# Masked-score products of a state-space mixer: two heads alternating, piece by piece, in place of one head at a time

## Chip, cores and metric

The kernel runs on one core of a Trainium2 chip, in one launch. The metric is the device time of one execution in microseconds; the time of a kernel is the median of its runs.

## What is computed

A block of two layers on 512 tokens (256 of context, 256 latent) of width 1024, each layer a mixer and a convolutional feed-forward network. The first mixer is gated linear attention beside an mLSTM, the second, where the change lies, a bidirectional state-space mixer: 32 heads of 64 channels in 4 groups, whose B and C have a state of 128. Cut to what matters:

```python
def odd_mixer(hc, hl, ...):
    fc = odd_features(hc, ...)          # z, x, B, C, dt of the context
    fl = odd_features(hl, ...)          # the same of the latent tokens
    yc, yl = bidir_scan(scan_f, scan_b, ...)
    ...
# one step of a scan, in one direction:
#   y[t] = sum over s <= t of (C[t] . B[s]) exp(cum[t] - cum[s]) dt[s] x[s]
#        + exp(cum[t]) C[t] . state
```

The kernel takes the 256 latent tokens as one piece in each direction. For a head, the masked scores times the decays form a matrix of keys by queries, and the values `dt[s] x[s]` (64 channels) are multiplied with it. This product is what the change reorders.

## The kernel before

The weights come as blocks of 128 x 128 in transfers of 1 MB on SyncE's queue. Each half of a transfer is split into a high part (ScalarE, L168) and a low part (VectorE or GpSimd, L169), and each block gives three products on TensorE (`mm3`, L180 to L182). The order of the work on each engine is the order in which a scheduler puts the program's instructions, from code written in stages.

`odd_mixer` (L921) works through the 32 heads in 16 chunks of two heads. Five stages run with lags, so that each step of the loop at L1134 holds parts of three chunks:

- `start` (step's own chunk) calls `project`: x through a convolution (ScalarE L949 and L952, VectorE L336, L337 and L953) and z through a gate (L1046, L1047); 16 blocks of weights, 48 products.
- `tokens` (the chunk before): x token-major (transposing products, L1057), weighted for the end state of the context (`xw`, L1062) and by dt (`xd`, L1063), the product for the end state (L1066) and its copy `S` (ScalarE, L1068).
- `outputs` (two chunks before): the products of masked scores with values (L1114), then VectorE adds the part from the end states and multiplies with the gate (L1116, L1117), and ScalarE squares (L1120) for the norm. The squares of a group of four chunks are summed by GpSimd (L1122); after the fourth they go through `colsum` (L127), Newton steps on VectorE and `spread` (L135).
- `decays` (the chunk before): the decays between tokens, `G`, on ScalarE (L1084, L1087) and VectorE (L1086, L1088), from rows that a transfer spreads over all partitions (L1077).
- `inter` (the chunk before): the products with the end states (L1100), then VectorE (L1101) and GpSimd (L1102, L1103).

`PARTS` (L25) lists the pieces of the causal matrices: a direction, the tile of 128 keys, and the queries from and to. Of the four pieces two have 256 queries and two have 128. In `outputs` each head has these four products; they add up in one region of PSUM, partitions 0 to 63 for the chunk's first head and 64 to 127 for its second, in a bank (`vps`) of which there is one only, and which `inter` uses too. The products of L1114 are of 128 keys by 64 channels, in plain float32.

Two other places matter below. `mod_part` (L243) computes shift and scale of a norm: eight products (L249), each with 32 output rows, and product k adds into the quarter k % 4 of the partitions. After the chunks come the high and low parts of y (L1143 on ScalarE, L1144 on VectorE) and the out-projection; where there is room the scheduler puts pieces of both beside the last chunks.

Of the kernel before, what the change touches and what calls it, by code (L numbers as in the profile page):

```python
# [16 lines left out]
P = 128  # L17
D = 1024
KD = 8
TL = 256  # L20
T = 512
SEGS = ((0, 0, 256), (1, 256, 512))
EPS = 1e-6
# causal pieces of a 256-token segment, keys in tile t: (direction, t, queries from, to, mask column, offset)
# [27 lines left out]
def block_kernel(ctx: ExitStack, tc: tile.TileContext, A: dict, out: bass.AP):  # L52
    nc = tc.nc
    PSUM = bass.MemoryType.PSUM
# [53 lines left out]
    def rsqrt(ss, scale, eps):  # L108
        """(ss * scale + eps) ** -0.5 of a few columns, by Newton steps from the exponent's halving"""
        n = ss.shape[-1]  # L110
        m, y, w = (np_.tile([P, 16], F32, tag=t, name=nm(t), bufs=2)[:, :n] for t in ("rm", "ry", "rw"))
        v.tensor_scalar(out=m, in0=ss, scalar1=scale, scalar2=eps, op0=ALU.mult, op1=ALU.add)
        v.tensor_scalar(out=w.bitcast(I32), in0=m.bitcast(I32), scalar1=1, scalar2=None, op0=ALU.logical_shift_right)
        v.tensor_scalar(out=y.bitcast(I32), in0=w.bitcast(I32), scalar1=-1.0, scalar2=1597463007.0, op0=ALU.mult, op1=ALU.add)
        for _ in range(3):
            v.tensor_tensor(out=w, in0=y, in1=y, op=ALU.mult)
            v.scalar_tensor_tensor(out=w, in0=w, scalar=-0.5, in1=m, op0=ALU.mult, op1=ALU.mult)
            v.scalar_tensor_tensor(out=y, in0=w, scalar=1.5, in1=y, op0=ALU.add, op1=ALU.mult)
        return y

    def colsum(sq, c=0, ps=None):
        """column sums of sq [128, n] with the columns on partitions: [128, n / 128] of a PSUM tile"""
        nt = sq.shape[-1] // P
        ps = vps() if ps is None else ps
        for t in range(nt):
            # each product overwrites all but the first column of the one before
            te.matmul(out=ps[:, c + t:c + t + P], lhsT=sq[:, t * P:(t + 1) * P], rhs=ones[:, :P], start=True, stop=True)  # L127
        return ps[:, c:c + nt]

    def spread(col, out):  # L130
        """out[:, t] = col[t % 128, t // 128] on every partition"""
        nt = col.shape[-1]
        ps = vps()[:, :nt * P]
        for t in range(nt):
            te.transpose(ps[:, t * P:(t + 1) * P], col[:, t:t + 1].to_broadcast([P, P]), ident)  # L135
        s.copy(out=out, in_=ps)

# [1 line left out]
    class Stream:  # L139
        def __init__(self, src, nblocks, fill=None, every=1, skip=0, ahead=1, pool=rawp, eng=lambda u: v):  # L140
            """fill: other work, one piece of it put ahead of every `every`-th transfer's products;
            ahead: how many splits run ahead of the products; eng: what computes the low parts"""
# [5 lines left out]
        def load(self, d):  # L148
            """transfer d to its place in SBUF"""
            if self.rawi != d:  # L150
                w = min(16, self.n - d * 16) * P
                self.raw = self.pool.tile([P, 2048], F32, tag="raw", name=nm("raw"))
                # the first transfer in halves, its second one with its split
# [30 lines left out]
    def gemm_f(st, b0, nk, acts, c0=0, c1=T, bank=gps, ks=None):  # L184
        """feature-major: [128 columns of W, tokens c0:c1]"""
# [7 lines left out]
    def gemm_k(st, b0, nk, acts, spans, pss=None, ks=None):  # L193
        """as gemm_f for a few column tiles at once (blocks [k][tile]), so that products start with the first k"""
# [12 lines left out]
    def gemm_t(st, b0, nk, acts, tiles):  # L207
        """token-major: [128 tokens, 512 columns of W] per token tile"""
# [21 lines left out]
    def mod_chunk(l, j, pool=rawp, psa=vps, tag="raw", n=2, bufs=None):  # L230
        """512 of the vectors' columns, their weights in n transfers"""
# [11 lines left out]
    def mod_part(q, pool, psa):  # L243
        """as mod_chunk, 256 columns of the first layer's mixer norm"""
# [8 lines left out]
    def mod_out(l, c, n, ps, psa):  # L253
        """add up the quadrants, with the columns on partitions: n tiles of 128 columns from tile c"""
# [10 lines left out]
        if i in (1, 4):  # L265
            # (1 + scale) * gain, in place of scale
# [4 lines left out]
    class Norm:  # L271
        """1 / rms over the features of tokens c0:c1, a feature tile at a time"""
# [17 lines left out]
        def cols(self):  # L290
            """[token % 128, token tile]"""
            return rsqrt(self.most, 1.0 / D, EPS)

        def row(self):
            """on all partitions, the tokens along the free axis"""
# [29 lines left out]
    # residual: x += gate * y  # L325
# [6 lines left out]
    def conv_side(y, ps, w0, w2):  # L332
        """the two outer taps of a width-3 convolution within each segment"""
# [12 lines left out]
    def warm(n, rhs):  # L346
        """products of ones, so that the tensor engine keeps its clock up while the first data come"""
# [3 lines left out]
    with tc.tile_pool(name="stp", bufs=6) as stp:  # L351
# [13 lines left out]
        def start(k, acts):  # L365
            # the first products run as their K tiles come, between the parts of shift and scale
# [35 lines left out]
    with ExitStack() as st:  # L402
# [6 lines left out]
        def turn(k):  # L409
            """the gain, then token-major"""  # L410
# [29 lines left out]
def even_mixer(E, st, acts, pss0, then):  # L440
# [52 lines left out]
    # log_sigmoid(x) = min(x, 0) - ln(1 + exp(-|x|)), each table loaded once  # L493
# [60 lines left out]
    # token-major columns: [t, tile, row of RQ], and the end-state weights of the context  # L554
# [30 lines left out]
    for j in range(2):  # L585
# [51 lines left out]
        # end state of the context, both directions  # L637
# [22 lines left out]
        # outputs, token-major, and their norm per head  # L660
# [28 lines left out]
    # q and k carry a factor 2 each from the tanh form of silu  # L689
# [4 lines left out]
    def head(h):  # L694
# [5 lines left out]
        # end state of the context: [k, value | norm] per direction  # L700
# [15 lines left out]
        for sg in range(2):  # L716
# [4 lines left out]
            # [s, t] weights: forward s0 -> t 0:256, s1 -> t 128:256; backward s0 -> t 0:128, s1 -> t 0:256  # L721
# [28 lines left out]
    def finish(h):  # L750
        # output gate (twice it), norm, transposed
# [53 lines left out]
def conv_ffn(E, st, l, acts, fill, then):  # L805
# [20 lines left out]
    def around(y, ps, ti):  # L826
        """the other taps"""
# [15 lines left out]
    # VectorE keeps to one operand from SBUF where GpSimd works beside it  # L843
# [3 lines left out]
    def project(j):  # L847
# [5 lines left out]
        elif not full:  # L853
            # a pair to a bank; the others hold sums of the down-projection
# [3 lines left out]
        else:  # L858
            # the down-projection takes the usual banks before the last two are through
# [9 lines left out]
    for hf in range(nh):  # L869
# [6 lines left out]
        for jj in range(per):  # L876
# [4 lines left out]
            # the down-projection's first columns, as far as their K tiles are there  # L881
# [4 lines left out]
            if jj == per - 2 and not full:  # L886
                # and a column more while the last pairs are convolved
# [25 lines left out]
        if full and last:  # L913
            # the last two a segment at a time, so that the next norm starts on the first
# [6 lines left out]
def odd_mixer(E, st, acts, then):  # L921
# [13 lines left out]
    # dt, B, C, B: the context first, C without it  # L935
# [8 lines left out]
    def conv_silu(b0, ti, out, c0):  # L944
        """out = 2 silu(conv + bias)"""
# [13 lines left out]
    def group(q):  # L959
# [5 lines left out]
        # x and B each carry a factor 2  # L965
# [6 lines left out]
        # [s, dir, 384]: forward s0 x t 0:256, s1 x t 128:256; backward s1 x t 0:256, s0 x t 0:128  # L972
# [12 lines left out]
    # softplus(x) = max(x, 0) + ln(1 + u), u = exp(-|x|), with the rounding of 1 + u put back  # L985
# [24 lines left out]
    # token-major: context w_end = exp(c_end - cum) dt [s, dir*32 + head]; latent cum and dt  # L1010
# [7 lines left out]
    tok = T_([P, 2, P], "tokc")     # [s, tile, cum (64) | dt (64)]  # L1018
# [33 lines left out]
    def tokens(i):  # L1052
        """token-major x: context weighted for the end state, latent by dt, per direction; D x"""
# [4 lines left out]
        xw = T_([P, 2, 2, 2, 64], "xw", pool=sp)    # [s, tile, dir, head, 64]  # L1058
        xd = T_([P, 2, 2, 2, 64], "xd", pool=sp)    # [s, dir, tile, head, 64]
# [13 lines left out]
    def decays(i):  # L1073
        """masked C B^T times the decays between tokens; the cumulative sums (negated) broadcast to all partitions"""
# [3 lines left out]
        G = T_([P, 2, 2, 384], "G", pool=sp)        # [s, dir, head, parts]  # L1078
# [15 lines left out]
    def inter(i):  # L1094
        """from the end states, each direction, times its decay since them"""
# [9 lines left out]
    def outputs(i):  # L1105
# [4 lines left out]
        for h in range(2):  # L1110
            r = slice(64 * h, 64 * h + 64)
            mm = [(xd[:, d, t, h, :], G[:, d, h, xo:xo + e - a], a, e) for d, t, a, e, mc, xo in PARTS]
            for n, (l, rr, a, e) in enumerate(mm):
                te.matmul(out=py[r, a:e], lhsT=l, rhs=rr, start=n == 0, stop=n == len(mm) - 1)  # L1114
        # times (twice) silu(z), square sum per group
# [41 lines left out]
def blocks_f(w, ms):  # L1157
    """feature-major blocks of w (K, M): for each column tile, its K tiles"""
# [3 lines left out]
def blocks_k(w, ms):  # L1162
    """feature-major blocks, for each K tile its column tiles"""
# [3 lines left out]
def blocks_kf(w):  # L1167
    """four column tiles together, then the other four one by one"""
# [3 lines left out]
def blocks_t(w, c0):  # L1172
    """token-major blocks: for each K tile, four column tiles from c0"""
# [11 lines left out]
def cols(vv):  # L1185
    """vector -> [128, n] with feature f at [f % 128, f // 128]"""
# [3 lines left out]
def layout(inp):  # L1190
# [40 lines left out]
    # even in-projection  # L1231
# [19 lines left out]
    # FFN  # L1251
# [11 lines left out]
    # odd in-projection  # L1263
# [12 lines left out]
    # constants of the shapes  # L1276
# [29 lines left out]
```

## Time and profile before

| | |
|---|---|
| time, median of 3 runs (lowest, highest) | 1298.69 us (1298.11, 1303.0) |
| profiled execution: span from first to last instruction | 1300.7 us |
| TensorE busy | 1245.6 us, 96% |
| VectorE busy | 942.7 us, 72% |
| ScalarE busy | 597.2 us, 46% |
| GpSimd busy | 381.4 us, 29% |
| HBM traffic | 146 GB/s over the span |
| products L1114 | 16 groups, the first from 834.76 us, the last to 1022.59 us |

The profile is of one execution of its own; nothing around its span is listed, so its time is taken as its span. It lies 2.0 us above the median of the runs. Products are pipelined: the record of one covers its fill and its drain, so that the records of neighbours overlap, and the distance of their starts tells the pace. A float32 product of this kind leaves two records, one for each pass. In the forms `128*64` is the part of the array that is used, rows by columns; `128x256` is the operand that streams through.

### The profile page before, as it was taken

Reading aid. Unit: us, or ns where it says so; the run is one execution under the profiler, and the core shown is the slowest. Engines: PE = TensorE matmul, PEld = TensorE weight load, DVE = VectorE, ACT = ScalarE, POOL = GpSimd, SP = SyncE. Lnnn points to the kernel's source line nnn. Section 1 sums busy time; section 2 is a strip of 40 time slices with the busy share of each in tenths; the row PEclk is TensorE's granted clock in tenths of the full one; section 3 lists DMA queues with packets and bytes.
Section 4 is the critical chain, followed back from the end, with each engine's and each line's share of the span. In section 5 each row is a group of like instructions: output and inputs, shape, how many; then the busy total and the mean of one; then the engine's idle time right before and its main releaser. Section 6 shows DMA issues by size and latency. Waiting matters only on the chain.

```text
span 1300.7 us, 19329 instructions
## 1 busy us (share of the span) xinstructions
PE 1245.6 (96%) x7358; PEld 1027.8 (79%) x7358; DVE 942.7 (72%) x2137; ACT 597.2 (46%) x947; POOL 381.4 (29%) x214
## 2 busy tenths in 40 slices
PE   7999999999999999999999998999999999899987
PEld 5557787876867777888888897888888888899987
DVE  4483899576659766237774488788888957999993
ACT  3463344343344433124442266565566545555553
POOL 0100000000226646136664000122222124678720
PEclk8999999999999999999999999999999998999999
DMA  9556303324445664232202136444363473545431
GB/s 373 184 190 230 117 12 111 109 89 165 166 175 213 254 232 135 98 123 97 98 33 98 65 106 175 130 153 131 114 152 105 153 251 132 207 164 181 156 130 66
DMA packets 39964, 190.96 MB, mean 147 GB/s; under 512 B 4592, under 2 KB 10552, under 8 KB 20928
## 3 DMA queue, kind: packets, MB, share of 16 engines
q1 hardware_dynamic: 36512, 185.48, 41.3%
q10 hardware_dynamic: 3360, 4.25, 1.1%
q8 instruction: 58, 0.95, 0.3%
q14 instruction: 34, 0.28, 0.1%
HBM read 188.51 MB, written 1.20 MB: 146 GB/s over the span
## 4 chain that ended last, share of the span: by engine, by line
PE 71%; DVE 19%; ACT 3%; issue 3%; DMA 3%; POOL 1%; SPq 0%; ACTq 0%; DVEq 0%; POOLq 0%
PE gps L180 14%; PE gps L181 13%; PE gps L182 13%; DVE y L829 6%; PE mps L180 4%; PE mps L182 4%; PE mps L181 4%; PE vps L239 3%; PE vps L1114 2%; DVE ml L897 2%; DVE y L893 1%; PE gps L215 1%; PE gps L217 1%; PE gps L216 1%; PE vps L1100 1%
## 5 line engine op out<-in xcount | busy, mean ns | idle before, releaser
L169 POOL TENSOR_TENSOR wl<-raw,wh 128x1024 fp32r<-128x1024 f32 x111 | 268.1, 2426 | 515.2 <-ACT wh L168 515.0
L168 ACT ACTIVATE wh<-raw 128x1024 fp32r<-128x1024 f32 x226 | 237.3, 1054 | 173.1 <-PE gps L182 107.3
L180 PE MATMUL gps<-hh,wh 128*128 128x512 f32 (+1 forms) x840 | 297.1, 355 | 7.1 <-ACT hh L316 5.4
L182 PE MATMUL gps<-hl,wh 128*128 128x512 f32 (+1 forms) x840 | 295.6, 354 | 1.6 <-DVE hl L318 1.6
L181 PE MATMUL gps<-hh,wl 128*128 128x512 f32 (+1 forms) x840 | 295.4, 352 | 0.4 <-DVE wl L169 0.3
L829 DVE SCALAR_TENSOR_TENSOR y<-mps,fcw,y 128x255 f32<-128x255 f32 (+3 forms) x576 | 223.0, 426 | 38.7 <-ACT y L823 32.5
L169 DVE TENSOR_TENSOR wl<-raw,wh 128x1024 fp32r<-128x1024 f32 x115 | 140.9, 1232 | 81.1 <-ACT wh L168 80.9
L180 PEld LDWEIGHTS gps<-hh,wh 128*128 128x128 f32 x840 | 159.5, 190 | 43.2 <-issue 12.1
L180 PE MATMUL mps<-hh,wh 128*128 128x256 f32 (+1 forms) x528 | 172.7, 327 | 10.9 <-DVE y L829 8.6
L182 PEld LDWEIGHTS gps<-hl,wh 128*128 128x128 f32 x840 | 160.0, 191 | 25.0 <-issue 4.2
L181 PEld LDWEIGHTS gps<-hh,wl 128*128 128x128 f32 x840 | 160.0, 191 | 23.6 <-issue 4.1
L181 PE MATMUL mps<-hh,wl 128*128 128x256 f32 (+1 forms) x528 | 171.1, 324 | 0.0
L182 PE MATMUL mps<-hl,wh 128*128 128x256 f32 (+1 forms) x528 | 171.1, 324 | 0.0
L180 PEld LDWEIGHTS mps<-hh,wh 128*128 128x128 f32 x528 | 101.0, 191 | 27.8 <-issue 9.3
L180 PE MATMUL gps<-mh,wh 128*128 128x256 f32 (+1 forms) x352 | 117.7, 334 | 2.7 <-ACT mh L896 2.7
L181 PE MATMUL gps<-mh,wl 128*128 128x256 f32 (+1 forms) x352 | 117.2, 333 | 0.0
L182 PE MATMUL gps<-ml,wh 128*128 128x256 f32 (+1 forms) x352 | 117.0, 333 | 0.0
L182 PEld LDWEIGHTS mps<-hl,wh 128*128 128x128 f32 x528 | 101.1, 192 | 7.4
L181 PEld LDWEIGHTS mps<-hh,wl 128*128 128x128 f32 x528 | 101.0, 191 | 7.3
L829 DVE SCALAR_TENSOR_TENSOR y<-gps,fcw,y 128x189 f32<-128x189 f32 (+3 forms) x196 | 83.2, 437 | 23.3 <-ACT y L823 19.4
L823 ACT ACTIVATE y<-mps,fcw 128x256 f32<-128x256 f32 (+1 forms) x66 | 40.6, 639 | 87.7 <-PE mps L182 87.7
L180 PEld LDWEIGHTS gps<-mh,wh 128*128 128x128 f32 x352 | 66.8, 190 | 10.0 <-ACT mh L896 2.9
(281 smaller groups left out, 1850.4 us busy)
## 6 DMA issues: line engine op xcount, KB each, us to landing
raw<-in_up SPq DMA_DIRECT2D x42, 1024.0 KB, 5.0
rawm<-in_modw SPq DMA_DIRECT2D x36, 1024.0 KB, 5.7
raw<-in_win SPq DMA_DIRECT2D x32, 1024.0 KB, 5.4
raw<-in_dn SPq DMA_DIRECT2D x20, 1024.0 KB, 5.0
raw<-in_wout SPq DMA_DIRECT2D x10, 1024.0 KB, 5.1
rawm<-in_mods SPq DMA_DIRECT2D x8, 1024.0 KB, 14.0
R<-crd SPq DMA_DIRECT2D x32, 256.0 KB, 4.5
rawm<-in_modw SPq DMA_DIRECT2D x8, 512.0 KB, 5.3
```

Source lines behind the costliest of these rows:

```text
L168: s.activation(out=hi[:, :n], in_=rw, func=AF.Copy)
L169: self.eng(u).tensor_tensor(out=lo[:, :n], in0=rw, in1=hi[:, :n].bitcast(F32), op=ALU.subtract)
L180: te.matmul(out=ps, lhsT=lhi, rhs=rhi, start=first, stop=False)
L181: te.matmul(out=ps, lhsT=llo, rhs=rhi, start=False, stop=False)
L182: te.matmul(out=ps, lhsT=lhi, rhs=rlo, start=False, stop=last)
L215: te.matmul(out=ps, lhsT=ah[:, sl], rhs=hi[:, c:c + 512], start=k == 0, stop=False)
L216: te.matmul(out=ps, lhsT=ah[:, sl], rhs=lo[:, c:c + 512], start=False, stop=False)
L239: te.matmul(out=ps[32 * (k % 4):32 * (k % 4) + 32, :], lhsT=spad[:, k, :], rhs=raw[:, kk * 512:(kk + 1) * 512], start=k < 4, stop=k >= 4)
L823: s.activation(out=y, in_=ps, func=AF.Identity, scale=fcw[:, ti * 10 + 4:ti * 10 + 5], bias=fcw[:, ti * 10 + 9:ti * 10 + 10])
L829: v.scalar_tensor_tensor(out=o, in0=i, scalar=fcw[:, ti * 10 + wi:ti * 10 + wi + 1], in1=o, op0=ALU.mult, op1=ALU.add)
L897: part = lambda ya=ya, h_=h_, l_=l_: ep.tensor_tensor(out=l_, in0=ya, in1=h_.bitcast(F32), op=ALU.subtract)
L1114: te.matmul(out=py[r, a:e], lhsT=l, rhs=rr, start=n == 0, stop=n == len(mm) - 1)
```

## The change

In `outputs` the two loops change places. Before, the loop over the two heads is outside and that over the four pieces inside, so that a head's four products follow each other; now the loop over the pieces is outside, and the two heads alternate. The products, their operands and their flags for starting and ending a sum are the same. Line 1114 is line 1113 in the new code. Comments are dropped all over the file, which changes no instruction.

```diff
@@ odd_mixer, outputs(i) @@
         py = ybank()[:, :256]
-        for h in range(2):
-            r = slice(64 * h, 64 * h + 64)
-            mm = [(xd[:, d, t, h, :], G[:, d, h, xo:xo + e - a], a, e) for d, t, a, e, mc, xo in PARTS]
-            for n, (l, rr, a, e) in enumerate(mm):
-                te.matmul(out=py[r, a:e], lhsT=l, rhs=rr, start=n == 0, stop=n == len(mm) - 1)
+        for n, (d, t, a, e, mc, xo) in enumerate(PARTS):
+            for h in range(2):
+                te.matmul(out=py[64 * h:64 * h + 64, a:e], lhsT=xd[:, d, t, h, :], rhs=G[:, d, h, xo:xo + e - a],
+                          start=n == 0, stop=n == len(PARTS) - 1)
         v.tensor_tensor(out=y2[i], in0=u, in1=py, op=ALU.add)
```

The order on TensorE in an ordinary step, from the last product of a projection (`gps`) over the transposing products to the first of the next projection; `xd` holds the values, `G` the masked scores, `vps` the sums:

```order
 L182 MATMUL gps_7049<-hl_6095,wh_7014 128x256
 L1057 MATMUL mps_7082<-c_104,xx_6897 128x128 x4
-L1114 MATMUL vps_7100<-G_6990,xd_6975 64x256
-L1114 MATMUL vps_7100<-G_6990,xd_6975 64x128 x2
-L1114 MATMUL vps_7100<-G_6990,xd_6975 64x256 x2
-L1114 MATMUL vps_7100<-G_6990,xd_6975 64x128 x2
-L1114 MATMUL vps_7100<-G_6990,xd_6975 64x256
+L1113 MATMUL vps_7100<-G_6990,xd_6975 64x256 x2
+L1113 MATMUL vps_7100<-G_6990,xd_6975 64x128 x4
+L1113 MATMUL vps_7100<-G_6990,xd_6975 64x256 x2
 L180 MATMUL gps_7137<-hh_6080,wh_7050 128x512
```

Before, the sizes run 256, 128, 128, 256 for the first head and the same for the second; now each size comes twice in a row, once for each head. What stands ahead of the group and behind it is as it was.

The last group but one, among products of the out-projection:

```order
 L1066 MATMUL mps_8872<-xw_8866,bt_1037_6496 128x256 x2
 L182 MATMUL gps_9005<-hl_8958,wh_9011 128x256
-L1114 MATMUL vps_8879<-G_8841,xd_8812 64x256
-L1114 MATMUL vps_8879<-G_8841,xd_8812 64x128 x2
-L1114 MATMUL vps_8879<-G_8841,xd_8812 64x256 x2
-L1114 MATMUL vps_8879<-G_8841,xd_8812 64x128 x2
-L1114 MATMUL vps_8879<-G_8841,xd_8812 64x256
+L1113 MATMUL vps_8879<-G_8841,xd_8812 64x256 x2
+L1113 MATMUL vps_8879<-G_8841,xd_8812 64x128 x4
+L1113 MATMUL vps_8879<-G_8841,xd_8812 64x256 x2
 L180 MATMUL gps_9006<-hh_8957,wh_9011 128x256
```

The same move, with the same neighbours. It happens 16 times; VectorE, ScalarE, GpSimd and SyncE have the same instructions in the same order before and after.

## Rows read from the trace of the kernel before

**Rows 1.** The page: span, TensorE's busy time, its granted clock in 40 slices.
```profile
span 1300.7 us, 19329 instructions
PE 1245.6 (96%) x7358; PEld 1027.8 (79%) x7358; DVE 942.7 (72%) x2137; ACT 597.2 (46%) x947; POOL 381.4 (29%) x214
PEclk8999999999999999999999999999999998999999
```
**Rows 2.** Steps of the chunk stage: busy time of each engine, granted clock, DMA.
```profile
core 0: us, PE busy (x) PEld busy (x) DVE busy (x) ACT busy (x) POOL busy (x), PEclk, DMA share, GB/s
834.76:847.72 12.96, 12.96 (x78) 10.82 (x77) 9.83 (x19) 7.75 (x14) 2.92 (x2) 1.00 0.50 153
...
1014.73:1020.43 5.70, 5.70 (x42) 4.84 (x41) 5.70 (x10) 4.01 (x6) 1.53 (x3) 1.00 0.00 1
```
**Rows 3.** Groups by shape, 834 to 1024 us: busy us, mean ns of one.
```profile
L1114 PE MATMUL vps<-G,xd 128*64 128x256 f32 x128 | 32.8, 392 | 0.0
L1114 PEld LDWEIGHTS vps<-G,xd 128*64 128x64 f32 x256 | 24.5, 136 | 6.7 <-issue 2.6 <-DVE G L1086 0.2
L1114 PE MATMUL vps<-G,xd 128*64 128x128 f32 x128 | 19.2, 273 | 0.0
L1066 PE MATMUL mps<-xw,bt 128*128 128x256 f32 x60 | 15.4, 378 | 0.0
L1057 PE MATMUL mps<-c,xx 128*128 128x128 f32 x60 | 9.0, 272 | 0.0
```
**Rows 4.** TensorE's timeline, one group and its neighbours: start us, us, what.
```profile
847.19 0.60 PE L1057 MATMUL mps<-c,xx 128*128 128x128 f32 x4
847.72 2.22 PE L1114 MATMUL vps<-G,xd 128*64 128x256 f32 x16
...
849.56 0.38 PE L1114 MATMUL vps<-G,xd 128*64 128x256 f32 x1
849.87 0.50 PE L180 MATMUL gps<-hh,wh 128*128 128x512 f32 x1
...
851.14 1.02 PE L1066 MATMUL mps<-xw,bt 128*128 128x256 f32 x4
```
**Rows 5.** Shift and scale (L249): one group's timeline, its busy time, its durations.
```profile
18.58 1.07 PE L249 MATMUL mps<-rawm,spad 128*32 128x256 f32 x16
...
18.58:19.65 1.07, 1.07 (x16) 0.42 (x16) 1.00 1.03 436
...
L249 PE MATMUL mps<-rawm,spad x128: 379/379/636, 14.8 to 48.0; 128*32 128x256 f32 x128
```
**Rows 6.** Waits, 834 to 1024 us: us in total, times, longest us.
```profile
ACT G L1084 <- PE vps L1114: 16.5, 14, 1.5
...
PEld vps L1100 <- ACT S L1068: 2.0, 10, 0.2
```
**Rows 7.** Timeline of VectorE and ScalarE behind that group.
```profile
849.51 0.41 DVE L1062 TENSOR_TENSOR xw<-mps,wet 128x256 f32<-128x256 f32 x1
...
849.98 1.71 ACT L1084 ACTIVATE G<-R,tokc 128x256 f32<-128x256 f32 x4 [1.17 <-PE vps L1114]
...
852.20 0.37 ACT L1068 COPY S<-mps 128x256 f32<-128x256 f32 x1
...
852.70 1.06 PE L1100 MATMUL vps<-cl,S 128*128 128x256 f32 x4
...
858.27 0.75 DVE L336 SCALAR_TENSOR_TENSOR t<-gps,c,t 128x510 f32<-128x510 f32 x1 [2.13 <-ACT t L949]
```
**Rows 8.** Timeline behind the fourth group: the norm's column sums.
```profile
879.65 0.71 PE L127 MATMUL vps<-ones,t 128*128 128x128 f32 x4 [0.20 <-POOL t L1122]
```
**Rows 9.** Timeline behind the last three groups.
```profile
1009.83 1.71 ACT L1084 ACTIVATE G<-R,tokc 128x256 f32<-128x256 f32 x4 [0.29 <-PE vps L1114]
...
1014.53 2.64 DVE L1144 SCALAR_TENSOR_TENSOR hl<-y,c,hh 128x256 fp32r<-128x256 f32 x4
1017.09 0.41 DVE L1116 TENSOR_TENSOR y<-u,vps 128x256 f32<-128x256 f32 x1
...
1020.02 3.47 DVE L1144 SCALAR_TENSOR_TENSOR hl<-y,c,hh 128x256 fp32r<-128x256 f32 x5
1023.42 0.41 DVE L1116 TENSOR_TENSOR y<-u,vps 128x256 f32<-128x256 f32 x1
...
1027.07 0.71 PE L127 MATMUL vps<-ones,t 128*128 128x128 f32 x4 [0.60 <-POOL t L1122]
```

## The prediction

> **What bounds the kernel now.** I read the page first: TensorE (PE) is busy for 96% of the span and its granted clock is at the upper level nearly everywhere [rows 1]. A share over the whole span says nothing about one stage, so I then cut the stage that the change touches, the state-space chunks from 834.76 to 1022.59 us, into its steps, each from one group of masked-score products (L1114) to the next [rows 2]. In an ordinary step PE is busy for all 12.96 us at a clock of 1.00 (2.4 GHz) while VectorE (DVE) works 9.83 us and ScalarE (ACT) 7.75 us: this stage is bound by PE. In the step that begins with the fifteenth group DVE too is busy for all 5.70 us, so there a saving on PE need not count.
>
> Next I looked at how fast one group runs. The groups by shape [rows 3] count 256 records for the 128 products, so each product is two passes. A pass of 256 columns is recorded with 0.392 us and one of 128 columns with 0.273 us, but these overlap; the pace has to be read from rows of several passes. Four passes of 128 columns (L1057) last 0.60 us, which with 0.272 for a single one leaves 0.11 us from one start to the next; four of 256 columns (L1066) last 1.02 us with 0.378 for one, so 0.215 us [rows 3, 4].
>
> One head of a chunk has two products of 256 columns and two of 128, that is four passes of each length: 4 x 0.215 + 4 x 0.11 = 1.30 us. Two heads end to end are 2.60 us. The group's surroundings add some: the last pass starts at 849.56 and the next stream's first product at 849.87 [rows 4], 0.31 us later, 0.095 more than the pass itself. Its start costs about 0.05, by the next row. So without any overlap a group would take 2.60 + 0.05 + 0.095 = 2.74 us to the next product. Measured: from 847.72 to 849.87, 2.15 us. So the two heads overlap for 0.59 us already, the second head's start beside the first head's end; the first 0.7 us of the group and the last run on one half of the array's columns (the form is 128*64).
>
> That alternating helps is shown elsewhere in the same trace. The shift-and-scale products (L249) go round four quarters of the output's partitions, product by product, and the row of 16 passes of 256 columns lasts 1.07 us [rows 5]. One after another they would take 16 x 0.215 = 3.4 us; four quarters side by side take 4 x 0.215 = 0.86. With the last pass's record (0.379) counted by its pace (0.215) the row is 0.91 long, so 0.05 is what the start cost.
>
> **The change, part by part.** It removes and adds no product, and no instruction of another engine moves. In each of 16 groups the eight products alternate between the two heads: sizes 256, 256, 128, 128, 128, 128, 256, 256, so that the heads run in lock step.
>
> Group: 1.30 us for both heads together, 0.05 for the start, 0.095 to the next product, makes 1.44 to 1.45 us. Against 2.15 this is 0.70 us less on PE per group.
>
> Does that reach the end? ACT's first decay instruction (L1084) waits for the group's end, and is followed by the copy of the end states (L1068), whose result the next products (L1100) want at once: 852.20 + 0.37, then 852.70 [rows 6, 7]. ACT was idle for 1.17 us before L1084, more than 0.70, so this chain comes forward by the whole amount. The products L1066 need DVE's second L1062, which ends at 849.92, while PE comes to them at 851.14; 1.22 us to spare becomes 0.52. DVE's first job of the next projection waits 2.13 us for ACT, which waits for PE [rows 7], so DVE has air too, and the price of this cover being gone would be PE waiting where it now has 0.52 to spare. Every fourth step holds the norm of a group of chunks, where PE waits 0.20 us for GpSimd's sum [rows 8]. That sum hangs on ACT's work behind L1084 and so comes forward with it. I count 0.70 in all steps up to the thirteenth group: 13 x 0.70 = 9.1 us.
>
> The last three differ. At the fourteenth ACT was idle only 0.29 us before L1084 [rows 9], so L1100 comes forward by 0.29. At the fifteenth DVE is in 2.64 us of low parts (L1144) and takes the sum (L1116) only at 1017.09, though the group ended before; L1100 writes the bank that L1116 reads, so PE meets that wait. At the sixteenth 3.47 us of the same hold L1116 until 1023.42, and the products L127 already wait 0.60 us for what follows from it [rows 9]. For these two I count nothing (between 0 and 0.70 each). Sum: 9.1 + 0.3 = 9.4 us.
>
> Past the stage PE runs on with the out-projection and the feed-forward; weight transfers there are triggered by buffers that PE frees, so they shift with it. I count no change.
>
> The profiled execution has a span of 1300.7 us, 2.0 above the median of the runs (1298.69), inside their spread. Its span would become 1291.3, and the median run 1298.69 - 9.4 = **1289.3 us**, 0.72% less. About 0.5% (6.5 us, that is below 1292.2) is what a measurement of this kernel can tell from no change.
>
> **The rivals.** *Passes start in program order.* If a pass could start only once every pass before it in the program has started, the second head's product would lag by one pass, 0.215 us: a group takes 1.66 us, 0.49 saved, 13 x 0.49 + 0.3 = 6.7 us and 1292.0 us. Rows against it: by such an order head 1 could not start before head 0's last pass (at 0.05 + 1.30 - 0.215 = 1.13 us), and the group of before would take 1.13 + 1.30 + 0.095 = 2.53, not 2.15 [rows 4]; and L249's row, at one pass of 0.215 us behind the other for each of 8 products, would be about 2.1 us long and not 1.07 [rows 5]. The Trainium skill states such a rule (TensorE: Matmul & The Clock Gate, Part 3: Packing small matmuls): matmuls start and end strictly in program order, and only weight loads are pulled ahead. By that rule the change would bring some 6.7 us; the trace of this kernel disagrees in both places. Chance 0.07, half of it on either side of the bound.
>
> *The gain is eaten.* Weight loads could be the limit: 16 of them at 0.136 us are 2.18 us [rows 3], just what a group takes, and if they ran one at a time nothing would be gained (1298.7). Against it: L249's 16 weight loads keep the loader busy for only 0.42 us together [rows 5], so loads for different parts of the columns run beside each other. More likely a handover such as ACT's copy to L1100, which already keeps PE's loads waiting 2.0 us in ten steps [rows 6], or DVE's 0.52, gives back half: 16 x 0.35 = 5.6 us, 1293.1 us. Chance 0.11.
>
> *Slower: each change of half empties the array.* If the first pass of one head began only when the other's had run out, the present overlap of 0.59 us would go: 2.74 us a group, and 13 to 16 groups x 0.59 = 7.7 to 9.4 us, so 1306.4 to 1308.1. It decides where one head's first pass starts: inside the other's product or after it. The overlap of 0.59 already there and L249 speak against it; for it speaks only that these products use halves where L249 uses quarters. Chance 0.04.
>
> That the change doesn't do what it says I rule out: the program's order on PE has the heads alternating, and the rest as it was.
>
> **How the numbers follow.** 0.78 for the forecast, 0.07, 0.11 and 0.04 for the rivals. Faster by over 0.5%: 0.78 + 0.04 = 0.82; within: 0.11 + 0.03 = 0.14; slower: 0.04. Low end of the range: all 16 groups give 0.70, 11.2 us, and a run lies 0.6 us below the median as the lowest does: 1286.9, taken as 1286.5. High end: the gain half eaten (1293.1) and the spread of the runs, 1295.0.
>
> **What would show it.** In the changed kernel's timeline the row of 16 passes of such a group should be 1.5 us long in place of 2.2, and the next product should start 1.45 us after its first; ordinary steps should be 12.25 us long in place of 12.96, with PE still busy throughout. ACT should be idle about 0.5 us before L1084 in place of 1.17. The last two steps should shrink least. If groups take 1.66 the order of passes decides; if they take 1.45 and the steps are not shorter, a wait in front of L1066 or L1100 took the gain; if they take 2.2 or more, weight loads or a drain did.

## Result and the profile after

| | before | changed |
|---|---|---|
| time, median of 7 runs each (lowest, highest) | 1302.11 us (1297.91, 1303.0) | 1293.67 us (1289.39, 1296.69) |
| ratio, 95% interval | | 0.9942 [0.9927, 0.9958] |
| profiled execution: span | 1300.7 us | 1289.4 us |
| profiled execution: device time | | 1291.57 us |
| TensorE busy | 1245.6 us | 1233.4 us |
| first group of L1114 (now L1113) to the last | 185.68 us | 177.00 us |

By the medians the kernel became 8.4 us faster (0.65%); the ratio over all runs, 0.9942, says 0.58%. It is faster, since the whole interval lies below 1; that it is so by more than the bound of 0.5% isn't shown, since the far end of the interval is a gain of 0.42%. The forecast was 1289.3 us and a gain of 9.4 us, the range 1286.5 to 1295.0. The page of the changed kernel, against [rows 1]:

```profile
span 1289.4 us, 19329 instructions
PE 1233.4 (96%) x7358; PEld 1016.6 (79%) x7358; DVE 942.9 (73%) x2137; ACT 596.9 (46%) x947; POOL 385.3 (30%) x214
PEclk9989999999999999999999999999999999999999
```

PE's busy time fell by 12.2 us, more than the stage did, and as many instructions ran. Of the 12.2 us, 10.2 lie in the stage, where PE's idle time grew by 1.5 us; 2.0 lie behind it, where the granted clock was 0.97 before and 0.98 now. One group in PE's timeline, against [rows 4]:

```profile
845.66 1.52 PE L1113 MATMUL vps<-G,xd 128*64 128x256 f32 x16
847.11 0.50 PE L180 MATMUL gps<-hh,wh 128*128 128x512 f32 x1
...
848.39 1.02 PE L1066 MATMUL mps<-xw,bt 128*128 128x256 f32 x4
```

The row of 16 passes is 1.52 us long in place of 2.22, and the next product starts 847.11 - 845.66 = 1.45 us after the first, in place of 2.15. By the single records the two heads' passes start 6 to 7 ns apart all through the group. By shape, against [rows 3], the busy time of the passes fell from 32.8 and 19.2 to 20.1 and 9.7 us, while one pass lasts as long as before:

```profile
L1113 PE MATMUL vps<-G,xd 128*64 128x256 f32 x128 | 20.1, 392 | 0.0
L1113 PEld LDWEIGHTS vps<-G,xd 128*64 128x64 f32 x256 | 14.8, 136 | 5.2 <-issue 2.6 <-DVE G L1086 0.2
L1113 PE MATMUL vps<-G,xd 128*64 128x128 f32 x128 | 9.7, 273 | 0.0
```

The steps of the stage, against [rows 2] (same columns): an ordinary one, one with a norm, the one behind it, and those that begin with the fourteenth and fifteenth group:

```profile
845.66:857.90 12.24, 12.24 (x77) 10.21 (x76) 9.83 (x19) 7.76 (x14) 4.08 (x3) 1.00 0.44 150
870.16:884.55 14.39, 13.54 (x84) 11.02 (x83) 12.62 (x36) 8.44 (x16) 1.69 (x2) 1.00 0.32 113
884.55:896.53 11.98, 11.98 (x76) 10.02 (x75) 11.16 (x18) 7.51 (x13) 3.66 (x4) 1.00 0.46 151
...
998.35:1004.89 6.54, 6.54 (x48) 5.41 (x47) 6.22 (x19) 6.54 (x16) 1.06 (x2) 1.00 0.56 182
1004.89:1010.41 5.52, 5.25 (x43) 4.30 (x42) 5.52 (x9) 4.06 (x6) 1.35 (x3) 1.00 0.00 1
```

The same steps of the kernel before that [rows 2] don't hold (norm, the one behind it, fourteenth):

```profile
873.61:888.30 14.69, 14.27 (x85) 11.62 (x84) 12.63 (x36) 8.44 (x16) 1.28 (x2) 1.00 0.33 111
888.30:901.00 12.70, 12.70 (x76) 10.63 (x75) 11.17 (x18) 7.52 (x13) 3.65 (x4) 1.00 0.43 141
...
1007.57:1014.73 7.16, 7.16 (x48) 5.97 (x48) 6.13 (x19) 6.84 (x17) 0.97 (x2) 1.00 0.58 167
```

An ordinary step, and the one behind a norm, gave 0.7 us each (ten of them). **The norm's step gave only 0.30**: PE is idle in it for 14.39 - 13.54 = 0.85 us, where it was idle for 0.42. The fourteenth step gave 0.6, the fifteenth 0.2. Together 10 x 0.70 + 3 x 0.30 + 0.61 + 0.19 = 8.7 us, the whole difference of the stage.

What happened in the norm's step is in the timelines. Before (its group starts at 873.61):

```profile
877.51 1.21 DVE L169 TENSOR_TENSOR wl<-raw,wh 128x1024 fp32r<-128x1024 f32 x1
...
878.86 0.74 POOL L1122 TENSOR_TENSOR t<-t,t 128x256 f32<-128x256 f32 x1 [8.36 <-ACT t L1120]
```

After (its group starts at 870.16):

```profile
874.06 1.21 DVE L169 TENSOR_TENSOR wl<-raw,wh 128x1024 fp32r<-128x1024 f32 x1
...
874.71 1.15 POOL L1122 TENSOR_TENSOR t<-t,t 128x256 f32<-128x256 f32 x1 [7.66 <-ACT t L1120]
...
875.92 0.71 PE L127 MATMUL vps<-ones,t 128*128 128x128 f32 x4 [0.62 <-POOL t L1122]
```

VectorE's low part (L169) starts 3.90 us after its group in both kernels, since VectorE was busy up to there. GpSimd's sum (L1122) started 5.25 us after its group and starts 4.55 us after it now, 0.70 earlier as forecast. But it used to start when L169 had ended (877.51 + 1.21 = 878.72), and now lies beside its last 0.56 us, and takes 1.15 us in place of 0.74. The 0.41 more is what PE's wait in front of L127 grew by, from 0.20 [rows 8] to 0.62. Counted from the group, the sum ended after 5.25 + 0.74 = 5.99 us and ends after 4.55 + 1.15 = 5.70 us now: 0.29 earlier, which is what the step gave. The waits of PE over the stage say the same; before:

```profile
PE vps L127 <- POOL t L1122: 1.2, 4, 0.6
PE vps L135 <- DVE ry L118: 0.7, 3, 0.3
PE gps L181 <- DVE wl L169: 0.3, 1, 0.3
```

and after:

```profile
PE vps L127 <- POOL t L1122: 2.5, 4, 0.6
PE gps L181 <- DVE wl L169: 1.1, 1, 1.1
PE vps L135 <- DVE ry L118: 0.7, 3, 0.2
PE vps L1100 <- ACT wh L168: 0.3, 1, 0.3
```

The second row of after is the last group's saving: from that group to the last L127 it was 1027.07 - 1020.43 = 6.64 us before [rows 9]; it is 6.75 now (1010.41 to 1017.16). PE is through 0.7 us earlier and waits 0.8 us more for VectorE's low part of a weight block. Elsewhere hardly a wait took the place of what was saved (the last row's 0.3 us, in the fifteenth step): ACT's idle time in front of L1084 fell from 1.17 us [rows 7] to 0.47, and `S` is copied for L1100 in time:

```profile
847.23 1.71 ACT L1084 ACTIVATE G<-R,tokc 128x256 f32<-128x256 f32 x4 [0.47 <-PE vps L1113]
...
849.45 0.37 ACT L1068 COPY S<-mps 128x256 f32<-128x256 f32 x1
```

### The profile page after: what moved, and what is told of

It reads as the page before. It is cut to its first block, busy times and chain, and to the rows that moved or that the text cites. A ratio compares the mean times of both kernels' runs of the same rounds, so it can differ in the third digit from the quotient of the medians.

```text
span 1289.4 us, 19329 instructions
## 1 busy us (share of the span) xinstructions
PE 1233.4 (96%) x7358; PEld 1016.6 (79%) x7358; DVE 942.9 (73%) x2137; ACT 596.9 (46%) x947; POOL 385.3 (30%) x214
## 4 chain that ended last, share of the span: by engine, by line
PE 70%; DVE 19%; issue 4%; ACT 3%; DMA 3%; POOL 1%; SPq 0%; ACTq 0%; DVEq 0%; POOLq 0%
PE gps L180 13%; PE gps L181 13%; PE gps L182 13%; DVE y L829 6%; PE mps L180 5%; PE mps L182 4%; PE mps L181 4%; PE vps L239 3%; DVE ml L897 2%; PE vps L1113 1%; PE gps L215 1%; PE gps L216 1%; PE gps L217 1%; DVE y L893 1%; PE vps L1100 1%
## 5 line engine op out<-in xcount | busy, mean ns | idle before, releaser
L169 POOL TENSOR_TENSOR wl<-raw,wh 128x1024 fp32r<-128x1024 f32 x111 | 268.1, 2425 | 514.7 <-ACT wh L168 514.5
L169 DVE TENSOR_TENSOR wl<-raw,wh 128x1024 fp32r<-128x1024 f32 x115 | 140.9, 1232 | 79.5 <-ACT wh L168 79.3
```

The costliest lines, as they stand in the source:

```text
L169: self.eng(u).tensor_tensor(out=lo[:, :n], in0=rw, in1=hi[:, :n].bitcast(F32), op=ALU.subtract)
```

## Experiments

All start from the changed kernel; each diff is against it. The first three ask why alternating is worth 0.70 us a group: is it enough that heads change often (a queue of a few passes for each half), or must a pass wait for all before it?

**Alternating after every two products.**

```diff
-        for n, (d, t, a, e, mc, xo) in enumerate(PARTS):
+        for n0 in (0, 2):
             for h in range(2):
+                for n in (n0, n0 + 1):
+                    d, t, a, e, mc, xo = PARTS[n]
...
```

> The heads alternate after every two products instead of after every one. Theory Q (each half of the columns has a short queue of its own, in which three passes can wait: in the kernel before, head 1's first pass starts at 0.71 us, just when head 0's fifth of eight passes starts): four passes of head 0 are taken at once, head 1 starts within 0.05 us of head 0, a group takes 1.45 us to the next product and an ordinary step 12.25 us, as in the changed kernel. Rival S (the order must alternate product by product, since only the next product is looked at): head 1 starts no sooner than head 0's third pass, 0.48 us, so a group takes about 1.9 us and an ordinary step 12.7 us.

Measured: 1292.8 us, the kernel before 1296.49 beside it (one run each). A group in PE's timeline:

```profile
834.92 1.57 PE L1115 MATMUL vps<-G,xd 128*64 128x256 f32 x16
836.42 0.50 PE L180 MATMUL gps<-hh,wh 128*128 128x512 f32 x1
```

A group takes 1.50 us, 0.05 more than product by product; head 1's first pass starts 13 ns after head 0's, though four passes stand ahead of it in the program. Passes of one half need not have started before those of the other half behind them, and the rival's 1.9 us is out. The 0.05 us more were not foretold: head 1's sixth pass starts 0.154 us after its fifth, where 0.109 is the pace.

**One head at a time, the long products first.**

```diff
-        for n, (d, t, a, e, mc, xo) in enumerate(PARTS):
-            for h in range(2):
+        for h in range(2):
+            for n, p in enumerate((0, 3, 1, 2)):
+                d, t, a, e, mc, xo = PARTS[p]
...
```

> One head at a time as before, but each head's two products of 256 queries first and then its two of 128. Theory Q (three passes wait, the fourth blocks): head 1 starts when head 0's fifth pass does, now at 0.92 us and not at 0.71, since the four passes ahead are long ones; a group takes 2.36 us and an ordinary step 13.17 us, slower than before by 0.21 us each. Rival T (the second head starts a fixed time of 0.7 us after the first, whatever the sizes): 2.15 us and 12.96 us as before.

Measured: 1309.18 us (1296.49 beside it, one run each).

```profile
851.02 2.44 PE L1114 MATMUL vps<-G,xd 128*64 128x256 f32 x16
853.39 0.50 PE L180 MATMUL gps<-hh,wh 128*128 128x512 f32 x1
```

The group takes 2.37 us, 0.22 more than before, though products and heads are the same (2.36 was expected). By the single records head 1 starts 0.920 us after head 0, when head 0's fifth pass starts (0.914); in the kernel before it started at 0.707, and head 0's fifth pass at 0.701. With the long products first, head 0's fifth pass comes 0.21 us later, and head 1 with it. All three orders fit one account: the second head starts as soon as no more than three passes of the first still wait. That three is read from these starts and is no more than that; what holds the passes isn't shown.

**Alternating in chunks 3, 7, 11, 13, 14 and 15 alone**, to see whether steps add up or an early gain is given back later.

```diff
+        order = [(n, h) for n in range(4) for h in range(2)]
+        if i not in (3, 7, 11, 13, 14, 15):
+            order = [(n, h) for h in range(2) for n in range(4)]
...
```

> The heads alternate only in the groups of chunks 3, 7, 11 (behind which the norm's sums come) and 13, 14, 15; in the other ten they follow each other as before. If each step's gain is its own, as the two traces say, the three norm steps take 14.4 us and the last three 6.55, 5.5 and 6.0, while the ten others stay at 12.95 (12.7 after a norm), and from the first group to the last it is 1.7 us less than before (185.67), about 184.0 us. If instead the norm steps lost because the steps ahead of them had become shorter and had left work over, they gain the full 0.7 here and take 14.0 us, and the whole is about 182.8 us.

Measured: 1298.04 us in one run, 1296.49 beside it, which tells nothing apart; the steps do:

```profile
846.83:859.80 12.97, 12.97 (x78) 10.82 (x77) 9.83 (x19) 7.74 (x14) 3.65 (x3) 1.00 0.44 142
872.77:887.17 14.40, 13.53 (x85) 11.02 (x84) 12.63 (x36) 8.44 (x16) 1.73 (x2) 1.00 0.31 113
...
1005.80:1012.34 6.54, 6.54 (x48) 5.42 (x47) 6.21 (x19) 6.54 (x16) 1.05 (x2) 1.00 0.62 183
```

From first to last group 184.00 us, as foretold. A norm's step gives its 0.30 and no more even where the steps before it are untouched: what it lacks is decided inside that step. The run with alternating by two products says the same: its norm's step, too, is 14.40 us long, though its group takes 0.05 us more. The sum starts 0.05 us later there, lasts 1.10 us and ends 5.70 us after the group's start, as in the changed kernel.

**The sum in front of the norm left out** in the step in question.

```diff
-        if i % 4:
+        if i % 4 in (1, 2):
...
```

> As the changed kernel, but GpSimd's addition of the squares is left out behind every fourth chunk (the sums over a norm's group lack their first three chunks; the rest is computed as it was). Theory A (the norm steps gained 0.30 and not 0.70 us because the products L127 wait for this addition, which now falls into a VectorE operation of 1.21 us and takes 1.15 us instead of 0.74): L127 waits no more, and a norm step takes 13.8 us or less instead of 14.39. Rival B (VectorE's Newton steps, behind L1088 in its queue, set the length of the step): 14.2 to 14.4 us, with the wait moved from L127 to L135.

Measured: 1288.06 us in one run, 174.23 us from first to last group.

```profile
869.89:883.38 13.49, 13.49 (x84) 11.08 (x83) 12.67 (x35) 8.44 (x16) 0.43 (x1) 1.00 0.43 120
```

The step is 0.90 us shorter and PE is never idle in it. So the idle time hung on this sum and what comes from it: the wait in front of L135 went too, not only the 0.62 in front of L127. This run takes away the whole sum, not only its slowness. That VectorE makes it slow is seen by comparing such sums in the chunk stage of all eleven traces. With nothing on VectorE, or with L1062, L1063 or L1101, which read one operand from PSUM, they took 0.72 to 0.75 us. Those that started while VectorE was at L169 or L1144, which read two operands from SBUF, took 0.90 to 1.39 us and ended 0.58 to 0.60 us after that instruction. One, in the run that follows, had an L1144 and three L169 in a row beside it; it took 4.47 us and ended 0.60 us after the last of them.

**Whole width: no overlap possible.** Each product takes both heads' 128 columns of weights and writes all rows, so that nothing can run side by side.

```diff
-        for n, (d, t, a, e, mc, xo) in enumerate(PARTS):
-            for h in range(2):
-                te.matmul(out=py[64 * h:64 * h + 64, a:e], lhsT=xd[:, d, t, h, :], rhs=G[:, d, h, xo:xo + e - a],
+        for h in range(2):
+            for n, (d, t, a, e, mc, xo) in enumerate(PARTS):
+                te.matmul(out=py[:, a:e], lhsT=xd[:, d, t].rearrange("p h n -> p (h n)"), rhs=G[:, d, h, xo:xo + e - a],
...
```

> One head at a time with the products of before, but each takes the values of both heads as its 128 weight columns and writes all 128 rows, so that no two products can stand side by side (the second head's sums overwrite the first's, and half of each product is of no use). My sum: sixteen passes one behind the other, 4 x 0.215 + 4 x 0.11 for each head, 2.74 us from a group's first product to the next stream's, 0.59 more than before and 1.29 more than in the changed kernel; an ordinary step takes 13.55 us. Rival: the overlap of before is one of the records only (a start noted early), and the group takes 2.15 us and the step 12.95 here too.

Measured: 1309.18 us in one run, beside a median of 1301.07 us in 11 runs of the kernel before.

```profile
845.07 2.79 PE L1113 MATMUL vps<-G,xd 128*128 128x256 f32 x16
847.70 1.03 PE L1066 MATMUL mps<-xw,bt 128*128 128x256 f32 x4
...
845.07:858.37 13.30, 13.30 (x78) 11.67 (x77) 9.98 (x19) 7.63 (x14) 3.62 (x3) 1.00 0.50 140
```

Serial, the group is 2.63 us and not 2.74, and the step 13.30 and not 13.55. Both are longer than before (2.15 and 12.96), so the overlap in the kernel before was real and not one of the records only. Its size is not the difference of 2.63 - 2.15 = 0.48 us, since groups of half width pay for what this one doesn't. By the single records of the second group, each head's second pass follows its first after 0.267 us (0.218 here), the group starts 0.202 us after the last transposing pass (0.110 here), and the next product starts 0.309 us after the last pass (0.216 here, where it is L1066). Read from the starts in the kernel before, the overlap is 0.64 us: head 1 starts at 0.707, and head 0's last pass starts at 1.135 and takes 0.215. The Trainium skill (TensorEngine Tiling (Array Packing), Key Properties) says that a change of tiling mode, not of the tile alone, drains the engine; the trace fits this, with 0.09 us more to the next start at either end of a group and 7 ns from head to head inside. On TensorE (the second line), ScalarE and VectorE some instructions stand in another order in this kernel, so the step's 0.34 us can't be divided further.

Then to the 0.40 us that a norm's step lost. **The norm written behind `inter`.**

```diff
...
+
+    def norm(i):
         if i % 4 == 3:
...
-        for stage, lag in ((start, 0), (tokens, 1), (outputs, 2), (decays, 1), (inter, 1)):
+        for stage, lag in ((start, 0), (tokens, 1), (outputs, 2), (decays, 1), (inter, 1), (norm, 2)):
```

> The changed kernel with the norm's column sums, Newton steps and scaling written behind the products with the end states of the same step and not ahead of them. Theory A (0.4 to 0.9 us of each norm step are PE waiting at L127 for GpSimd's addition): L1100 and more of the projection stand ahead of L127 and cover the wait; the three norm steps take 13.5 to 13.9 us in place of 14.39, the others stay, and from the first group to the last it is 1.5 to 2.7 us less than 177.0. Rival: the only bank that L127, L135, L1100 and the groups use hands the wait on to the next user, and the steps stay within 0.2 us of the changed kernel's. In the time of a run 2 us are 0.15%, less than can be told.

Measured: 1291.83 us, median of 6 runs, ratio to before 0.9934 [0.9919, 0.9949]; 175.99 us from first to last group, 1.01 less where 1.5 to 2.7 were expected. Norm's step, the one behind it, and PE's waits:

```profile
870.81:884.61 13.80, 13.08 (x84) 10.88 (x83) 13.13 (x35) 8.31 (x16) 4.11 (x3) 1.00 0.41 137
884.61:896.86 12.25, 12.25 (x78) 10.21 (x77) 11.21 (x19) 7.56 (x14) 2.33 (x2) 1.00 0.37 121
```

```profile
PE vps L135 <- DVE ry L118: 2.2, 3, 0.7
...
PE vps L127 <- POOL t L1122: 0.6, 1, 0.6
```

The norm's step is 0.59 us shorter, as expected, but the step behind it is 0.27 us longer, which wasn't. The wait for GpSimd went, but the Newton steps on VectorE now stand right ahead of the products that need them: 0.7 us in each of three steps. A wait had only moved on.

**Sums behind `inter`, scaling a step later.** Column sums and Newton steps as in the run above, but `spread` and the scaling one step later, with that step's work between.

```diff
...
+
+    def sums(i):
+        if i % 4 == 3:
+            Z["n", i] = E.rsqrt(E.colsum(psq), 1.0 / 512, 4 * EPS)
+
+    def scale(i):
...
-            E.spread(E.rsqrt(E.colsum(sq), 1.0 / 512, 4 * EPS), r)
+            E.spread(Z.pop(("n", i)), r)
...
-        for stage, lag in ((start, 0), (tokens, 1), (outputs, 2), (decays, 1), (inter, 1)):
+        for stage, lag in ((start, 0), (tokens, 1), (outputs, 2), (decays, 1), (inter, 1), (sums, 2), (scale, 3)):
```

> As the kernel of e6, and the second half of the norm (L135 and the scaling) moved on into the next step, behind its products with the end states, so that VectorE's Newton steps have a whole step's time. Theory A (in e6 the wait went from L127 to L135, 0.7 us in each norm step, because the Newton steps stand behind L1088 in VectorE's queue): no wait of TensorE is left in steps 0 to 12; a norm step is an ordinary one and four passes of L127, 12.25 + 0.44 = 12.7 us, the step behind it 12.25 + 0.22 = 12.5 us, and from the first group to the last it is 175.99 - 2.6 = 173.4 us. Rival: the scaling's four operations on VectorE (1.4 us) now push back that step's own work, and it takes 13 us or more, so that less than 1 us is won. In the time of a run about 0.3% less than the changed kernel, ratio to before near 0.991; whether that can be told from the changed kernel is open.

Measured: 1288.44 us, median of 5 runs (1288.09 to 1290.49), ratio to before 0.9912 [0.9897, 0.9927] (1300.73 beside it); 173.30 us from first to last group, 173.4 expected.

```profile
870.98:883.69 12.71, 12.71 (x81) 10.65 (x80) 12.04 (x31) 7.42 (x13) 4.11 (x3) 1.00 0.46 148
883.69:896.16 12.47, 12.47 (x79) 10.33 (x78) 12.44 (x23) 8.55 (x16) 2.99 (x2) 1.00 0.43 145
```

PE is idle in neither step; together they are 25.18 us where the changed kernel has 14.39 + 11.98 = 26.37.

**The changed kernel again**, unedited, beside the whole-width and late-norm runs:

> The changed kernel once more. If the chunk stage alone differs, which is 8.67 us shorter in the trace (185.67 to 177.00 from the first group to the last), the ratio to before is 1 - 8.7 / 1302, 0.9933, within the spread of the runs; if the first comparison's 0.9942 is what reaches the end, something past the stage takes back about 1 us.

Measured: 1292.27 us (5 runs), ratio 0.994 [0.9926, 0.9955], 177.00 us from first to last group. And beside the last version:

> The changed kernel beside e8 on the same chip: 177.0 us from the first group to the last, ratio to before 0.994 as in the two comparisons already made.

Measured: 1292.84 us (6 runs, 1289.17 to 1295.9), ratio 0.9941 [0.9924, 0.9959], 177.00 us again. By the medians the split norm is thus 4.4 us (0.34%) faster than the change alone, of which 177.00 - 173.30 = 3.7 lie in the stage. The runs of the two overlap (two of the six lie below the other's highest, 1290.49), so of the 4.4 us only the stage's 3.7 is firm.

## Why the prediction was right, and where it was off

- *What bounds the stage.* Right: PE, in ordinary steps. What PE saved came out of the step, to 0.03 us.
- *The group, 1.44 to 1.45 us.* Right: 1.45. The overlap of before was put at 0.59; the starts put it at 0.64, since the 0.05 us for a start falls on each head and was counted once. The forecast didn't rest on that number, the slower rival's price did.
- *"I count 0.70 in all steps up to the thirteenth group: 13 x 0.70 = 9.1 us."* This is the step that failed. Ten gave 0.70, the three with a norm 0.30: 7.9 us. The reason given, that GpSimd's sum "comes forward with" ACT's work, held for its start but not for its end: 0.70 earlier it lies beside VectorE's L169, which did not move, and lasts 0.41 us longer. What the sum would lie beside in its new place had not been asked. The chunk-3-7-11 run shows the loss without any help from other steps, and leaving the sum out gives back more than it.
- *The last three: 0.29, 0, 0.* Too low by 0.5: they gave 0.61, 0.19 and, measured to the last L127, -0.11. In the fourteenth step PE had work throughout, so the wait counted on did not cap it at 0.29. For the last, "nothing" was right: a wait for VectorE's L169 rose from 0.25 to 1.07 us.
- *Sum of the stage.* 9.4 forecast, 8.7 measured: minus 1.2 for the norms, plus 0.5 for the tail.
- *Past the stage, no change.* No instruction there moved, but the rest of the program varies from run to run by more than it could be held to, so "no change" is neither shown nor contradicted: over the eleven profiled executions, whatever the kernel, first group 831.8 to 837.9 us after the start, last one 278.0 to 284.2 us ahead of the end. In the six runs beside the split norm the changed kernel's spans go from 1287.0 us at a mean granted clock of 0.993 to 1293.7 at 0.988.
- *The time itself.* 1289.3 against 1293.67. Of the 4.4 us, 3.4 are the starting point: the median of before was 1298.69 in three runs and 1302.11 in seven. The profiled execution held a sign of it: device time is 2.2 us above the span in the changed kernel, and if it was so before, a span of 1300.7 belongs to the run of 1303.0, not to one 2.0 us above the median. From that execution the sum would have been 1293.6. That the time came to lie within the range is owed to a high end that had been set by the half-eaten gain and the spread of the runs; by the time alone that rival, at 1293.1, would look like the winner. The steps tell the two apart.
- *The rivals.* "Passes start in program order" fell twice over: 7 ns between heads and 1.45 us here, and head 1's early start in pairs. The rule of the Trainium skill (TensorE: Matmul & The Clock Gate, Part 3: Packing small matmuls) that products start strictly in program order is not what this trace shows for products on different column halves: in the kernel before head 1's first pass starts at 0.707 us, and head 0's last three, which stand ahead of it in the program, at 0.81 to 1.135. "Each change of half empties the array" fell with the 7 ns. "The gain is eaten" happened in part: not in front of L1066 or L1100 as it said, but in front of L127, and for 1.2 us and not half. Weight loads were no limit: one at a time 256 of 0.136 us would be 34.8 us, and the loader was busy for 14.8.

Left open: why exactly three passes wait for each half, and what would have to move for the fifteenth and sixteenth steps, in which VectorE is busy without a gap, to give their 0.7 us. Neither was tried.

## What to carry to other kernels

Products that use a part of the array's columns ran side by side here only where the program alternates between the parts every few passes; a run of one part's products with the other's behind it overlapped at the seam alone. When a saving moves a chain forward, look at what each of its links will lie beside in the new place, and at the engine that does not come forward: here one GpSimd sum beside one VectorE instruction took back more than half of the gain of its step. And where a value goes through a chain of small steps on other engines before TensorE needs it, split the stage, so that a whole step of TensorE's work lies between asking and using.

## What the runs showed of the hardware

- Passes for different column halves of one accumulator need not start in program order: the second half's first pass started 0.707, 0.920, 0.013 and 0.007 us after the other half's first, by the order alone.
- GpSimd's addition of 128x256 took 0.74 us with VectorE idle and 1.15 us with 0.56 us of it beside VectorE's 128x1024 subtraction of two SBUF operands (L169); 1.15 - 0.56 = 0.59 us alone means that hardly 0.15 us' worth was done in the overlap, while VectorE kept its 1.21 us. The Trainium skill (GPSIMD Engine Reference, Specifications) says that GpSimd shares its SBUF interfaces with VectorE and contends with instructions of two SBUF inputs; this trace agrees and gives the price.
- The price fell on the one that started second. In the step behind a norm a GpSimd addition of the same size (L1102) starts 0.03 us ahead of L169; it keeps its 0.75 us, and L169 takes 1.79 us in place of 1.21 (changed kernel; the same before):

```profile
890.23 0.75 POOL L1102 TENSOR_TENSOR CE<-CE 128x256 f32<-128x256 f32 x1 [4.29 <-DVE CE L1101]
890.26 1.79 DVE L169 TENSOR_TENSOR wl<-raw,wh 128x1024 fp32r<-128x1024 f32 x1
```

- A change between half and whole width costs about 0.09 us to the next start at each end of a group.
- The stage repeats to 0.01 us between executions (177.00 three times), while the time around it moves by several us, in the six runs of one comparison along with the granted clock. For an edit inside such a stage its own length tells more than a median of the whole.
